# First retention head: values and gates as seven half products round the queries' second turn, weight sums by adding transfers, rotation in other tiles

## The chip, the cores and the metric

The kernel runs on one core of a Trainium2 chip. The metric is the device time of one execution in microseconds; the median of three runs is given. A core has engines that work side by side, each through its own list of instructions in order: TensorE (PE, matmuls; PEld is its weight load), VectorE (DVE), ScalarE (ACT), GpSimd (POOL) and SyncE (SP). The last two serve here to issue transfers, and a transfer issued by POOL may add to what lies at its destination. Engines wait for one another by semaphores.

## The reference

Two layers over 512 rows of 2048 values: forgetting attention with 16 heads, then retention with 8 heads, each with a gate, an output projection, a residual and a layer norm. The change lies in the second layer, at its first head:

```python
def retention_branch(x, w_in, w_out):
    proj = jnp.einsum('bsd,de->bse', x, w_in)
    q, k, v, gate = jnp.split(proj, [RET_QK_WIDTH, 2 * RET_QK_WIDTH, 2 * RET_QK_WIDTH + RET_V_WIDTH], axis=-1)
    q = rotary(q.reshape(B, S, RET_HEADS, RET_QK_DIM))
    k = rotary(k.reshape(B, S, RET_HEADS, RET_QK_DIM)) * (RET_QK_DIM ** -0.5)
    ...
    o = group_norm_heads(o).reshape(B, S, RET_V_WIDTH)
    y = o * jax.nn.silu(gate)
    return jnp.einsum('bse,ed->bsd', y, w_out)
```

Left out above: per head, scores q k^T times a decay, causal, times v, computed by chunks with a running state. A head has 256 columns each of queries and keys and 512 each of values and gates; the input is the normalised output of the first layer, 512 x 2048.

## The kernel before

**Products.** Every projection is a product of the 512 x 2048 input with a block of weights, 2048 x 512 for queries and keys of a head ("narrow") and 2048 x 1024 for gates and values ("wide"). Input and weights are cut into quarters: a11, a12, a21, a22 by half of the rows and half of the 2048 terms, the weights by half of the terms and half of the columns. Each operand is split into a coarse part h and a remainder l (`split`, L303: a ScalarE copy, then a VectorE subtraction), and a product is three matmuls (`mm3`, L308).

**Two kinds of unit.** `Plain` (L643) computes the four result quarters as eight half products. `Unit` (L364) needs seven, p1 to p7, with sums of the input's quarters (the forms s1 to s4, table `FORM`, L38) and of the weights' quarters. Its sums of weights are a chain in one tile of the ring q: quarter 11 for p1, then 12 is added for p5, 22 for p6 and 21 for p4; p7 takes 12 + 22. These additions are VectorE instructions on loaded tiles (`Block.add`, L553). In between results are kept: p2 and p1 (tile k0), p5 (k1) and p1 with p6, called u2, are copied out of their banks by ScalarE (`keep`, L395) and corrected on VectorE when p1, p3 and p7 end (`after`, L430). A half product is four blocks if wide and two if narrow; a wide block is twelve matmuls with 512 columns, a narrow one 24 with 256. In `Plain` each half product is half a result quarter's sum, and wide weights are loaded and split for each half of the rows anew.

**Order.** `Order` (L88) writes out the order of all instructions when the kernel is built. For each block (`slot`, L186) it issues loads up to nine blocks ahead, additions three ahead, splits two ahead and then the block's matmuls. Everything else is a task, a chain of steps; after each block the tasks get one step each (more if a step says wait=0) as long as the planned work of VectorE and ScalarE stays under a limit (L77). Tiles and banks are counted in rings (L74); where a block needs one that isn't free, `require` (L161) forces tasks on until it is. Three accumulators (two banks each) are b0, b1, b2; a unit calls them x, y, z: p1, p6, p7, p4 in x, p2 in y, p5 and p3 in z (`BANK`, L41).

**Around head 0.** The layer norm between the layers ends in `to_columns` (L1424), for each half of the rows: normalise, transpose on TensorE, scale and shift on ScalarE and VectorE, split. The first half gives a11 and a12, the second a21 and a22; the second half's rows are ready only while head 0's first products run. `combine` (L750) splits a21 and a22 and makes s1, s2, s4 and s3, the last only when the second half's plain products have used a21, whose tiles s3 takes (`left_half`, L661). The two banks of queries and keys are copied into tiles in0 and in1 (`take_qk`, L1556), which the last rows of the layer norm hold until their columns are done.

Head 0 has two `Plain` units; they run as queries and keys of the first half of the rows, values and gates of it, queries and keys of the second half, values and gates of it (L1775 to L1778). From head 1 on both are `Unit`s. `attend` (L1579) rotates queries and keys (10 VectorE instructions, two splits), computes scores, multiplies them by the decay table and splits the result; then `take_vg` (L1666) splits the value halves, and `retain` (L1694) does the rest. Tile g2, after head 0's rotation, becomes the room: one half is a fourth tile for raw weights, the other is tile y0 (`split_room`, L333). Head 1's queries use k1 for p1 and p5 and y0 for u2.

Of the kernel before, what the change touches and what calls it, by code (L numbers as in the profile page):

```python
# [11 lines left out]
F32 = mybir.dt.float32  # L12
# [218 lines left out]
def trunk(ctx: ExitStack, tc: tile.TileContext, xq, x, fb_f, columns, wf_in, narrow, wide, ln_g, ln_b, rot, decay,  # L231
# [132 lines left out]
    class Unit:  # L364
# [3 lines left out]
        def __init__(self, w, n, sink, rows=True, u2="k0", p1="k0"):  # L368
# [5 lines left out]
            self.early = False  # L374
# [7 lines left out]
        def accumulator(self, b):  # L382
            if self.tags is None:
                self.tags = dict(zip("xzy", banks))
                banks[:] = banks[1:] + banks[:1]
# [8 lines left out]

        def keep(self, what, bank):  # L395
            n = self.shape[2]
            if self.wide or what == "u2":
                tag = {"p1": self.p1, "p2": "k0", "p5": "k1"}.get(what, self.u2) if self.wide else self.u2
                require(lambda: free[tag])
                take(tag)  # L400
                if tag == "y0":
                    self.pair = in_room(0, [P, 1 if self.wide else 2, 2, n])
                    t = self.pair[:, 0]
                else:
                    t = pool.tile([P, 2, n], F32, name=what, tag=tag)
            else:
                tag = "k1"
                if what == "p1":
                    require(lambda: free[tag])
                    take(tag)  # L410
                    self.p15 = pool.tile([P, 2, 2, n], F32, name="p15", tag=tag)
                    self.p15_users = 2
                t = self.p15[:, int(what == "p5")]
# [73 lines left out]
        def run(self, order=ORDER, then={}, leaves=False, last=False):  # L487
# [6 lines left out]
            i = order.index(("p3", self.blocks - 1))  # L494
# [11 lines left out]
    class Block:  # L506
        before = None

        def __init__(self, unit, p, c, e, shares, shared, then_block, then_product, turned=False):
# [43 lines left out]
        def add(self):  # L553
# [9 lines left out]
            elif p in ("p5", "p6", "p4") and not self.sums:  # L563
# [7 lines left out]
        def split(self):  # L571
# [22 lines left out]
            if p == "p4":  # L594
                give("q")
            if u.early and p == "p6":
# [153 lines left out]
    def combine(rest, plain):  # L750
# [13 lines left out]
        for name in ("s1", "s2"):  # L764
# [10 lines left out]
            if name == "s1":  # L775
                give("g2")
# [747 lines left out]
    class Head:  # L1524
        def __init__(self, h):
# [14 lines left out]
        def first_vg(self, m, n, tile, done):  # L1540

            if m:
                return self.take_vg(m, n, tile, done)
            tag = ("k0", "k1")[n]

            def copy():
                yield need(act=0.97, **{tag: 1})
                take(tag)
                t = pool.tile([P, 2, 512], F32, name="vg_raw", tag=tag)
                nc.scalar.activation(t, tile, AF.Copy)  # L1550
                done()
                self.take_vg(m, n, t, lambda after=0: give(tag, after))

            spawn(copy(), 0)
# [375 lines left out]
```

## Time and profile before

| | before |
|---|---|
| median of three runs (2388.37 to 2389.93) | 2389.52 us |
| the profiled execution | 2388.19 us |
| its span, first to last instruction | 2386.4 us |
| granted clock of TensorE, mean | 0.995 |
| head 0, first value-and-gate block to head 1's first block | 1004.87 to 1127.09 us |
| head 1's stretch | 1127.09 to 1257.82 us |

The profile is of one execution. Rows of engines are: start or count, busy time, line, operation, tile written and tiles read, shape. "[1.23 <-ACT raw L1478]" is idle time of the engine before the instruction and what ended it. Matmuls overlap, so their mean length is longer than the time that one more of them takes. The rows that carry the argument are in the prediction.

### The profile page before, as it was taken

What the parts mean: (1) busy time and instruction counts of PE and PEld (TensorE: products, weight loads), DVE (VectorE), ACT (ScalarE), POOL (GpSimd) and SP (SyncE); (2) the same over time, 40 slices, a digit from 0 to 9 for tenths busy, and PEclk for the clock granted to TensorE, in tenths of its full rate; (3) what the DMA queues carried; (4) which work ended last, traced back from release to release, by engine and by line L of the source; (5) the groups of instructions that cost most, each with busy time, mean ns of one, the idle gap of its engine ahead of it and who ended that gap; (6) DMA issues with size and microseconds to landing.
All of it is one profiled execution on the core that took longest, in us unless ns stands there. A gap on an engine that the chain in (4) does not pass through costs nothing.

```text
span 2386.4 us, 34361 instructions
## 1 busy us (share of the span) xinstructions
PE 2320.9 (97%) x13144; PEld 2016.2 (84%) x13144; DVE 1892.1 (79%) x2480; ACT 1223.0 (51%) x1777; POOL 150.4 (6%) x236
## 2 busy tenths in 40 slices
PE   9999999999999999999999999999999999999995
PEld 9888798798799778788989898988889898777784
DVE  5888778778765655677888888888888889988887
ACT  4546556555554534564454535454545446544533
POOL 0000000000000000000010101010101001011002
PEclk9999999999999999999999999999999999999998
DMA  6355444544544457556675857575655659689778
GB/s 225 123 196 175 163 161 165 183 161 159 190 153 147 135 194 253 190 177 200 203 239 189 247 192 219 198 206 181 212 195 195 211 169 273 212 267 300 238 245 191
DMA packets 185140, 473.26 MB, mean 198 GB/s; under 512 B 18032, under 2 KB 63232, under 8 KB 184464
## 3 DMA queue, kind: packets, MB, share of 16 engines
q1 hardware_dynamic: 161440, 403.68, 50.8%
q0 software_dynamic: 23536, 67.39, 10.7%
q8 instruction: 103, 1.69, 0.3%
q14 instruction: 61, 0.50, 0.1%
HBM read 413.30 MB, written 61.91 MB: 199 GB/s over the span
## 4 chain that ended last, share of the span: by engine, by line
PE 57%; DVE 8%; issue 3%; DMA 3%; ACT 3%; POOL 0%; ACTq 0%; SPq 0%; DVEq 0%; POOLq 0%
PE acc L311 17%; PE acc L312 17%; PE acc L310 17%; DVE w_l L306 3%; ACT w_h L305 2%; PE mmp L310 1%; DMA w_raw<-in_wide 1%; PE mmp L311 1%; PE mmp L312 1%; DVE w_q L565 1%; DMA v_sum<-in_wide 1%; PE mmp L1202 1%; PE mmp L1736 0%; DMA y_s<-ny 0%; DVE z L1835 0%
## 5 line engine op out<-in xcount | busy, mean ns | idle before, releaser
L310 PE MATMUL acc<-w_h,a 128*128 128x512 f32 (+1 forms) x1616 | 581.7, 360 | 5.5 <-DVE p L460 2.9
L311 PE MATMUL acc<-w_l,a 128*128 128x512 f32 (+1 forms) x1616 | 575.9, 356 | 3.7 <-DVE w_l L306 3.7
L312 PE MATMUL acc<-w_h,a 128*128 128x512 f32 (+1 forms) x1616 | 575.6, 356 | 0.0
L305 ACT ACTIVATE w_h<-w_q 128x1024 fp32r<-128x1024 f32 x344 | 363.9, 1059 | 406.3 <-DVE w_q L565 229.2
L306 DVE TENSOR_TENSOR w_l<-w_raw,w_h 128x1024 fp32r<-128x1024 f32 x337 | 411.6, 1222 | 200.9 <-ACT w_h L305 199.6
L305 ACT ACTIVATE w_h<-w_raw 128x1024 fp32r<-128x1024 f32 x337 | 356.3, 1059 | 378.1 <-PE acc L312 171.2
L306 DVE TENSOR_TENSOR w_l<-w_q,w_h 128x1024 fp32r<-128x1024 f32 x344 | 420.1, 1222 | 93.9 <-ACT w_h L305 86.7
L311 PE MATMUL acc<-w_l,s 128*128 128x512 f32 (+1 forms) x1344 | 485.5, 361 | 9.1 <-DVE w_l L306 8.9
L310 PE MATMUL acc<-w_h,s 128*128 128x512 f32 (+1 forms) x1344 | 489.3, 364 | 1.8 <-ACT w_h L305 1.6
L312 PE MATMUL acc<-w_h,s 128*128 128x512 f32 (+1 forms) x1344 | 483.9, 360 | 0.0
L310 PEld LDWEIGHTS acc<-w_h,a 128*128 128x128 f32 x1616 | 305.5, 189 | 48.8 <-issue 4.2
L311 PEld LDWEIGHTS acc<-w_l,a 128*128 128x128 f32 x1616 | 305.7, 189 | 47.7 <-DVE w_l L306 7.0
L312 PEld LDWEIGHTS acc<-w_h,a 128*128 128x128 f32 x1616 | 305.4, 189 | 44.0
L311 PEld LDWEIGHTS acc<-w_l,s 128*128 128x128 f32 x1344 | 254.4, 189 | 51.5 <-DVE w_l L306 16.6
L310 PEld LDWEIGHTS acc<-w_h,s 128*128 128x128 f32 x1344 | 254.4, 189 | 38.0 <-ACT w_h L305 2.1
L312 PEld LDWEIGHTS acc<-w_h,s 128*128 128x128 f32 x1344 | 254.2, 189 | 38.1
L565 DVE TENSOR_TENSOR w_q<-w_q,w_raw 128x1024 f32<-128x1024 f32 x218 | 265.4, 1220 | 9.6 <-DMA w_raw<-in_wide 7.2
L310 PE MATMUL acc<-a,w_h 128*128 128x256 f32 x464 | 131.5, 283 | 1.3 <-ACT w_h L305 1.3
L312 PE MATMUL acc<-a,w_l 128*128 128x256 f32 x464 | 131.6, 284 | 0.8 <-DVE w_l L306 0.8
L311 PE MATMUL acc<-a,w_h 128*128 128x256 f32 x464 | 131.3, 283 | 0.0
L312 PE MATMUL acc<-s,w_l 128*128 128x256 f32 x448 | 126.8, 283 | 0.0
L311 PE MATMUL acc<-s,w_h 128*128 128x256 f32 x448 | 126.7, 283 | 0.0
(244 smaller groups left out, 2942.5 us busy)
## 6 DMA issues: line engine op xcount, KB each, us to landing
w_raw<-in_wide SPq DMA_DIRECT2D x343, 512.0 KB, 3.9
w_raw<-in_narrow SPq DMA_DIRECT2D x146, 512.0 KB, 3.9
w_q<-in_wide SPq DMA_DIRECT2D x60, 512.0 KB, 4.3
room<-in_wide SPq DMA_DIRECT2D x45, 512.0 KB, 4.4
w_q<-in_narrow SPq DMA_DIRECT2D x26, 512.0 KB, 4.3
y_s<-ny POOLq DMA_DIRECT2D x48, 256.0 KB, 7.3
y_s<-y POOLq DMA_DIRECT2D x40, 256.0 KB, 6.2
room<-in_narrow SPq DMA_DIRECT2D x16, 512.0 KB, 4.6
```

The costliest lines, as they stand in the source:

```text
L305: nc.scalar.activation(h, src, AF.Copy)
L306: nc.vector.tensor_sub(l, src, f32(h))
L310: nc.tensor.matmul(ps, a[0], b[0], start=start, stop=False, skip_group_check=True)
L311: nc.tensor.matmul(ps, a[0], b[1], start=False, stop=False, skip_group_check=True)
L312: nc.tensor.matmul(ps, a[1], b[0], start=False, stop=stop, skip_group_check=True)
L565: nc.vector.tensor_add(u.chain[c], u.chain[c], t)
L1202: nc.tensor.matmul(ps[:, k * P:], vh[:, k], pT[:, k, k * P:], start=k == 0, stop=k == ST - 1)
```

## The change

Head 0's values and gates become a `Unit`. It runs in two parts: p2 and p1 after the queries' first turn, the other five after the second turn, p3 and p7 block by block in turn. `combine` follows the query unit. The accumulators of x and z change places in this unit (`between`). Its sums of weights for p5, p6 and p4 are adding transfers on POOL's queue straight from the weights in memory into the tile of ring q, each issued behind the split that last read it (`adds`); the sum for p7 stays on VectorE. The room is made as soon as s1 is split. Head 0's rotation has its tiles in the room and in four of the small ones, and its split queries in g0 and g1; the rotation's steps are cut smaller for all heads, the decay table is loaded ahead of the rotation, and the scores start two blocks sooner after it. Head 1's queries keep p1 and p5 in y0 and u2 in k1, and its values keep p5 in y0.

```diff
@@ Unit
-            self.early = False
+            self.early = self.between = self.adds = False
+            self.p15_tag = self.p5 = "k1"
...
             if self.tags is None:
-                self.tags = dict(zip("xzy", banks))
-                banks[:] = banks[1:] + banks[:1]
+                x, z, y = banks
+                if self.between:
+
+                    x, z = z, x
+                self.tags = dict(x=x, z=z, y=y)
+                banks[:] = z, y, x
...
+        def kept_tile(self, tag):
+            require(lambda: free[tag])
+            take(tag)
+            shape = [P, 2, 2, 256]
+            return in_room(0, shape) if tag == "y0" else pool.tile(shape, F32, name="kept", tag=tag)
+
         def keep(self, what, bank):
             n = self.shape[2]
             if self.wide or what == "u2":
-                tag = {"p1": self.p1, "p2": "k0", "p5": "k1"}.get(what, self.u2) if self.wide else self.u2
...
+                tag = {"p1": self.p1, "p2": "k0", "p5": self.p5}.get(what, self.u2) if self.wide else self.u2
+                t = self.kept_tile(tag)
...
             else:
-                tag = "k1"
+                tag = self.p15_tag
                 if what == "p1":
...
+                    self.p15 = self.kept_tile(tag)
...
-            i = order.index(("p3", self.blocks - 1))
+            i = order.index(("p3", self.blocks - 1)) if ("p3", 0) in order else 0
@@ Block
+            self.comes = u.adds and p in ("p5", "p6", "p4")
...
-            if not self.sums and not shared and p != "p1" and not (turned and p == "p3"):
+            if not self.sums and not self.comes and not shared and p != "p1" and not (turned and p == "p3"):
                 self.quarter = {"p2": "21", "p3": "22", "p4": "21", "p5": "12", "p6": "22", "p7": "12"}[p]
...
-            return -1 if p is None or self.sums or self.again else self.u.of[p, self.c].at
+            return -1 if p is None or self.sums or self.comes or self.again else self.u.of[p, self.c].at
...
-            elif p in ("p5", "p6", "p4") and not self.sums:
+            elif p in ("p5", "p6", "p4") and not self.sums and not self.comes:
                 t = u.lent.pop(("p2", c)) if self.shared else self.t
                 nc.vector.tensor_add(u.chain[c], u.chain[c], t)
...
             if p == "p4":
                 give("q")
+            elif u.adds and p in ("p1", "p5", "p6"):
+                q = {"p1": "12", "p5": "22", "p6": "21"}[p]
+                nc.gpsimd.dma_start(raw.rearrange("p a b -> p (a b)"), u.source(q, c), accum_op=ALU.add)
@@ combine
             if name == "s1":
-                give("g2")
+                if rest:
+                    split_room()
+                else:
+                    give("g2")
@@ Head.__init__ (first_vg goes altogether)
                 self.qk_unit = Plain(narrow, 8, self.take_qk, lambda: [banks[0]] * 2, rows=False)
-                self.vg_unit = Plain(wide, 6, self.first_vg,
-                                     lambda: {(m, n): banks[1 + n] for m in range(2) for n in range(2)})
             else:
                 self.qk_unit = Unit(narrow, 8 + h, self.take_qk, rows=False, u2="y0")
-                self.vg_unit = Unit(wide, 6 + h, self.take_vg, u2="k2")
...
+                if h == 1:
+
+                    self.qk_unit.u2, self.qk_unit.p15_tag = "k1", "y0"
+            self.vg_unit = Unit(wide, 6 + h, self.take_vg, u2="k2")
+            if h == 1:
+                self.vg_unit.p5 = "y0"
@@ Head.attend
         def attend(self):
-            yield need(tmp=4 if self.h == 0 else 2)
+            yield need(tmp=2 if self.h else 4)
             cos, sin = tmp("cos"), tmp("sin")
+            half = None if self.h else [tmp("rope_b") for _ in range(2)]
             nc.sync.dma_start(cos, rot[0])
             nc.sync.dma_start(sin, rot[1])
             by_half = lambda t: t.rearrange("p (m t) -> p m t", m=2)
-            tags = ("k2",) if self.h == 0 else ("in0", "in1")
-            tags_qk = ("g1", "g2") if self.h == 0 else ("g0", "g1")
-            yield need(wait=3, until=lambda: self.have == 4 and all(free[t] for t in tags_qk + tags))
-            for t in tags_qk + tags:
+            tags = ("y0",) if self.h == 0 else ("in0", "in1")
+            tags_qk = "g0", "g1"
+            yield need(wait=3, until=lambda: self.have == 4 and all(free[t] for t in tags_qk + tags + ("d0",)))
+            for t in tags_qk + tags + ("d0",):
                 take(t)
+            dec = pool.tile([P, S], F32, name="dec", tag="d0")
+            nc.sync.dma_start(dec, decay[self.h])
 
             qk = [pool.tile([P, 2, 1024], F32R, name=f"qk_{j}", tag=t) for j, t in zip("hl", tags_qk)]
-            if self.h == 0:
-                half = [by_half(tmp("rope_b")) for _ in range(2)]
-            else:
+            if self.h:
                 self.raw = self.qk_unit.p15, self.qk_unit.pair
 
             for j in range(2):
-                yield need(dve=1.75, wait=0)
+                yield need(dve=1.14, wait=0)
                 raw = self.raw[j]
-                a, *b = (pool.tile([P, 2, 2, 256], F32, name="rope", tag=t) for t in tags)
-                b = [b[0][:, :, e] for e in range(2)] if b else half
+                if self.h:
+                    a, b = (pool.tile([P, 2, 2, 256], F32, name="rope", tag=t) for t in tags)
+                    b = [b[:, :, e] for e in range(2)]
+                else:
+                    a, b = in_room(0, [P, 2, 2, 256]), [by_half(t) for t in half]
                 nc.vector.tensor_mul(a, raw, by_half(cos)[:, :, None, :].to_broadcast([P, 2, 2, 256]))
+                yield need(dve=0.6, wait=0)
                 nc.vector.scalar_tensor_tensor(b[0], raw[:, :, 1], -1.0, by_half(sin), op0=ALU.mult, op1=ALU.mult)
-                yield need(dve=1.85, wait=0)
+                yield need(dve=0.6, wait=0)
                 nc.vector.tensor_mul(b[1], raw[:, :, 0], by_half(sin))
                 for e in range(2):
+                    yield need(dve=0.6, wait=0)
                     nc.vector.tensor_add(a[:, :, e], a[:, :, e], b[e])
                 if j == 1:
-                    for _ in range(4 if self.h == 0 else 2):
+                    for _ in range(2 if self.h else 4):
                         give("tmp")
...
             for t in tags:
                 give(t)
-            yield need(d0=1, in0=1, in1=1)
-            for t in ("d0", "in0", "in1"):
+            yield need(in0=1, in1=1)
+            for t in ("in0", "in1"):
                 take(t)
...
-            dec = pool.tile([P, S], F32, name="dec", tag="d0")
-            nc.sync.dma_start(dec, decay[self.h])
...
-            i, last, wait = 0, [], 3
+            i, last, wait = 0, [], 1
...
             for t in tags_qk:
-                if t == "g2":
-                    split_room()
-                else:
-                    give(t)
+                give(t)
@@ the runs
     first = heads[0]
-    first.qk_unit.run(EACH[0], then={0: lambda: spawn(combine(True, first.vg_unit), 1)})
-    first.vg_unit.run(EACH_N[0])
+    first.qk_unit.run(EACH[0], then={0: lambda: spawn(combine(True, first.qk_unit), 1)})
+    first.vg_unit.between = first.vg_unit.adds = True
+    first.vg_unit.run(FIRST)
     first.qk_unit.run(EACH[1], then={len(EACH[1]) - 1: lambda: spawn(first.attend())})
-    first.vg_unit.run(EACH_N[1], then={len(EACH_N[1]) - 1: lambda: spawn(first.retain())})
+    first.vg_unit.run(REST, then={"p4": lambda: spawn(first.retain())})
```

More of the change, by code (lines that the diff above doesn't have):

```diff
@@ L397, in keep @@
             if self.wide or what == "u2":
-                tag = {"p1": self.p1, "p2": "k0", "p5": "k1"}.get(what, self.u2) if self.wide else self.u2
[L399 to L403, printed above, removed]
-                else:
-                    t = pool.tile([P, 2, n], F32, name=what, tag=tag)
+                tag = {"p1": self.p1, "p2": "k0", "p5": self.p5}.get(what, self.u2) if self.wide else self.u2
+                t = self.kept_tile(tag)
+                if self.wide:
+                    t = t.rearrange("p a b n -> p (a b n)").rearrange("p (a n) -> p a n", a=2)
+                else:
+                    self.pair = t
+                    t = t[:, 0]
             else:
-                tag = "k1"
+                tag = self.p15_tag
                 if what == "p1":
-                    require(lambda: free[tag])
-                    take(tag)
-                    self.p15 = pool.tile([P, 2, 2, n], F32, name="p15", tag=tag)
+                    self.p15 = self.kept_tile(tag)
                     self.p15_users = 2
@@ L1533, in __init__ @@
                 self.qk_unit = Plain(narrow, 8, self.take_qk, lambda: [banks[0]] * 2, rows=False)
-                self.vg_unit = Plain(wide, 6, self.first_vg,
-                                     lambda: {(m, n): banks[1 + n] for m in range(2) for n in range(2)})
             else:
                 self.qk_unit = Unit(narrow, 8 + h, self.take_qk, rows=False, u2="y0")
-                self.vg_unit = Unit(wide, 6 + h, self.take_vg, u2="k2")
[L1540 to L1554, printed above, removed]
+                if h == 1:
[3 more added lines that the diff above has]
+                self.vg_unit.p5 = "y0"
         def take_qk(self, m, n, tile, done):
```

## The prediction, made before the kernel was run

> **What bounds the kernel now.** I read the page first, then the stretches of the first two retention heads, then the waits inside the first one.
>
> ```profile
> span 2386.4 us, 34361 instructions
> PE 2320.9 (97%) x13144; PEld 2016.2 (84%) x13144; DVE 1892.1 (79%) x2480; ACT 1223.0 (51%) x1777; POOL 150.4 (6%) x236
> PE 57%; DVE 8%; issue 3%; DMA 3%; ACT 3%; POOL 0%; ACTq 0%; SPq 0%; DVEq 0%; POOLq 0%
> ```
>
> TensorE is busy nearly throughout and carries the chain that ended last, so a TensorE instruction that goes is worth its time, as long as nothing else is late in its stretch. The next view gives busy time by stretch: the first eight value-and-gate blocks of head 0, the next eight, the second query turn, the last sixteen blocks, then heads 1 and 2 (about 130 us each).
>
> ```profile
> core 0: us, PE busy (x) PEld busy (x) DVE busy (x) ACT busy (x) POOL busy (x), PEclk, DMA share, GB/s
> 1004.87:1034.22 29.35, 26.09 (x120) 19.34 (x118) 15.21 (x18) 19.82 (x34) 0.00 (x0) 1.00 0.43 143
> 1034.22:1057.33 23.11, 22.16 (x96) 18.12 (x97) 20.98 (x20) 16.14 (x18) 0.00 (x0) 1.00 0.63 202
> 1057.33:1080.36 23.03, 23.03 (x193) 23.03 (x192) 18.06 (x16) 11.30 (x11) 0.00 (x0) 1.00 0.56 186
> 1080.36:1127.09 46.73, 46.73 (x212) 38.95 (x211) 34.55 (x35) 23.67 (x25) 0.00 (x0) 1.00 0.67 219
> 1127.09:1257.82 130.73, 130.20 (x750) 114.79 (x749) 114.66 (x146) 63.57 (x75) 13.01 (x20) 1.00 0.67 215
> 1257.82:1388.00 130.18, 129.93 (x747) 114.47 (x746) 113.15 (x140) 63.38 (x74) 13.96 (x22) 1.00 0.68 217
> ```
>
> From 1057 to 1127 TensorE has no idle time at all. It loses time only before about 1036, where the normalised rows of the second half are still being turned into columns; the waits between 1004 and 1130, summed, say for whom:
>
> ```profile
> PE acc L311 <- DVE w_l L306: 1.9, 2, 0.9
> PE mmp L1460 <- ACT raw L1478: 1.6, 2, 1.2
> PE acc L310 <- ACT w_h L305: 0.7, 2, 0.4
> ```
>
> Those 4.2 us come from ScalarE and VectorE handing work to and fro in strict order. POOL has nothing to do from 1004 to 1127.
>
> **The change part by part.** I number head 0's blocks from 0 at 1004.87. Before: 0 to 15 wide, 16 to 23 the second query turn, 24 to 39 wide. After: 0 to 7 wide (p2, p1), 8 to 15 the query turn, 16 to 35 wide (p5, p6, p3 with p7, p4).
>
> *Products.* The head's values and gates are 32 blocks now and 28 after (seven products of four). The price of a block is in the groups between 1080.4 and 1115.7:
>
> ```profile
> L310 PE MATMUL acc<-w_h,a 128*128 128x512 f32 x52 | 20.2, 389 | 0.0
> L311 PE MATMUL acc<-w_l,a 128*128 128x512 f32 x52 | 20.2, 389 | 0.0
> L312 PE MATMUL acc<-w_h,a 128*128 128x512 f32 x52 | 20.2, 389 | 0.0
> ```
>
> Three lines of 52 are 156 matmuls in 35.3 us without idle time: 0.226 us each (the 389 ns overlap), and 2.72 us for a block of twelve. Four blocks are **10.9 us**, all taken from a stretch where TensorE never waits. A narrow block is 23.03 / 8 = 2.88 us.
>
> *A copy in the stretch that is late.* p2 ends after block 3 and is copied out of its bank by ScalarE at once (128x1024). The nearest row is the copy of a raw bank, which the change removes later on, where it was hidden:
>
> ```profile
> L1550 ACT ACTIVATE vg_raw<-acc x2: 1005/1006/1006, 1047.7 to 1058.5; 128x1024 f32<-128x1024 f32 x2
> ```
>
> It is queued ahead of the split of block 6, and from there to block 8 every split is just in time (the waits above). Its ends are 0 and 2.0 (if p1's addition on VectorE, 1.2 us, delays a split as well); I take **+1.0**.
>
> *The query turn finds its bank full.* Both query turns use one bank pair. The copies of the first turn come late, since their tiles are held until the columns are done:
>
> ```profile
> 1034.22 0.50 PE L310 MATMUL acc<-w_h,a 128*128 128x512 f32 x1 [0.43 <-ACT w_h L305]
> 1035.67 0.50 PE L311 MATMUL acc<-w_l,a 128*128 128x512 f32 x1 [0.95 <-DVE w_l L306]
> 1033.12 1.99 ACT L305 ACTIVATE w_h<-w_raw 128x1024 fp32r<-128x1024 f32 x2
> 1035.02 1.06 ACT L1573 ACTIVATE qk_raw<-acc 128x512 f32<-128x512 f32 x2
> ```
>
> Now block 8 is wide, has another bank, and loses 1035.67 - 1034.22 - 0.23 = 1.2 us inside to w_l. After, block 8 is the second turn's first and starts when the copies end, 1035.02 + 1.06 = 1036.1, with its w_l already there: 1.9 lost instead of 1.2, and a little for the handing over: **+0.8** (ends 0, if the copies come one place earlier, and 2.0, if they come behind one more split).
>
> *p5 finds the same bank full.* `between` gives p5 the bank of the queries, so it waits for the second turn's copies:
>
> ```profile
> 1080.36 0.40 PE L310 MATMUL acc<-w_h,a 128*128 128x512 f32 x1
> 1080.44 1.06 ACT L305 ACTIVATE w_h<-w_raw 128x1024 fp32r<-128x1024 f32 x1 [1.82 <-PE acc L311]
> 1081.41 1.06 ACT L1573 ACTIVATE qk_raw<-acc 128x512 f32<-128x512 f32 x2
> ```
>
> Today the next block starts at 1080.36 in other banks while ScalarE does a split and then the copies, up to 1082.47. Kept in this order, p5 starts 2.1 us late, with 0.1 for the handing over **+2.2**. Ends: 1.1 (no split in front) and 3.2 (two). Behind that wait on TensorE stand only p5's own blocks.
>
> *Adding transfers.* Twelve additions of weights for p5, p6 and p4 go to POOL's queue; SP issues 16 loads in place of 32. The only such transfers now are at the end of the kernel (the issues, the landings of w_q<-in_wide, a window there, and a step of the chain of waits there):
>
> ```profile
> w_raw<-in_wide SPq DMA_DIRECT2D x343, 512.0 KB, 3.9
> w_q<-in_wide POOLq DMA_DIRECT2D x4, 512.0 KB, 9.7
> v_sum<-in_wide POOLq DMA_DIRECT2D x4, 512.0 KB, 7.3
> DMA to landing us min/median/max: 6.8/9.7/11.5
> 2310.00:2320.00 10.00, 10.00 (x46) 8.16 (x44) 5.07 (x5) 2.57 (x4) 1.94 (x3) 1.00 1.03 340
> 2323.71 13.79 DMA v_sum<-in_wide
> ```
>
> The 6.8 to 11.5 us were taken with the DMA engines full (1.03); here their share is about 0.6. The narrowest place is p5 to p6, four blocks apart. A split starts when the block three ahead of it has ended, and both halves are done about 2.7 us later; the same tile's next split must start 1.06 us before its block, so 6 x 2.72 - 1.1 - 2.7 = 12.5 us are left for the transfer. I take **0**; ends 0 and 1.3 (a landing of 13.8, as in the last row). The four follow each other by a block, so a late one is paid once. p1 to p5 has the query turn between, p6 to p4 eight blocks. POOL's queue holds nothing else then, so its waits hold up nobody.
>
> By the Trainium skill ("SBUF — State Buffer", SBUF: two separate sides) a transfer issued from POOL cannot get its descriptors written while VectorE runs a two-port operation, and 0.62 us became 3.1 in its example; by that figure, an estimate, the slowest landing would be 11.5 + 2.5 = 14.0 and the sum 1.5 us worse. So far the trace speaks against it, as here:
>
> ```profile
> 1180.00:1200.00 20.00, 20.00 (x95) 16.51 (x94) 18.72 (x20) 13.49 (x18) 4.32 (x8) 1.00 0.55 193
> ```
>
> Eight issues took 4.32 us, 0.54 each, beside a VectorE that was busy 18.72 of 20.
>
> *VectorE and ScalarE.* Four pairs of splits go (w_h, w_l); four sums for p7 and three corrections with a bank (p1, p3, p7) come on VectorE, and three bank copies replace two on ScalarE.
>
> ```profile
> L306 DVE TENSOR_TENSOR w_l<-w_raw,w_h 128x1024 fp32r<-128x1024 f32 x32 | 39.1, 1224 | 16.7 <-ACT w_h L305 16.6
> ```
>
> From 1034.22 to 1127.09 VectorE works 20.98 + 18.06 + 34.55 = 73.6 of 92.9 us. After: 73.6 + 3 x 1.22 = 77.2 of 92.9 - 10.9 + 3.0 - 0.7 = 84.3, or 92%. Heads 1 and 2 run at 88% and 87% with 0.5 and 0.25 us of idle TensorE, so I take 0; beyond them the cover is thin (a rival below).
>
> *Forms.* p5, p6, p3 and p7 need s1, s2, s4 and s3, so far needed only by head 1. The second halves of s1 and s4 are split at
>
> ```profile
> 1046.22 1.22 DVE L306 TENSOR_TENSOR s<-raw,s 128x1024 fp32r<-128x1024 f32 x1
> 1074.09 1.22 DVE L306 TENSOR_TENSOR s<-raw,s 128x1024 fp32r<-128x1024 f32 x1
> ```
>
> that is in blocks 12 and 22: one step of the combining a block from block 8 on, sixteen in all. s3 no longer waits for the last wide blocks. So s1 is there by block 12 (needed 16), s2 by 16 (20), s4 by 22 (24), s3 by 24 (25): no wait, one block of room at the narrowest.
>
> *Rotation and scores.* The same VectorE instructions, other tiles, smaller portions; the decay table (256 KB on SP) is loaded ahead. They move from free blocks beside the full ones. The smaller portions, the earlier table and the two blocks less of pause hold for the later heads too, where TensorE idles so little that they can win almost nothing; I take 0 for all of it, with the cover as just said.
>
> **Sum:** -10.9 + 1.0 + 0.8 + 2.2 = **-6.9 us** on the profiled execution's 2388.19 us (span 2386.4 and 1.8 around): 2381.3. The median of the runs shown, 2389.52, lies 1.3 above that execution, so **2382.6 us**. The ends of the unknown terms give -10.9 + 1.1 = -9.8 and -10.9 + 2.0 + 2.0 + 3.2 + 1.3 = -2.4, or 2379.7 to 2387.1.
>
> **The rivals.**
>
> *Nothing of it is waited for.* ScalarE's copies fit into its idle time and the better supply of weights also takes away most of the 4.2 us of waits: -10.9 - 1 gives 2377.6; with p5's wait alone 2380. For it: ScalarE is busy 19.8 of 29.4 us. Against: its order is strict. 0.15.
>
> *VectorE becomes the bound.* If it can be used only to the 88% of head 1, 77.2 us take 87.7 instead of 84.3: 3.4 us, 2386.0. For it: in the stretch of p3 and p7 the rotation comes on top of splits and sums. Against: what is late can go on into head 1. 0.15.
>
> *The transfers are late, or the copies stand behind more.* The upper ends above, and landings some 3 us longer: 2385 to 2390. 0.1.
>
> *The saving moves.* TensorE gets to head 1 earlier and waits there for head 0's attention: 2389. 0.08.
>
> *Slower: head 1 stops at tile k1.* Head 1's queries put their p6 into k1, which is free only when head 0's second value half is split, after all rotation and scores. Today that takes from the first row to the end of the second:
>
> ```profile
> 1090.99 1.22 DVE L1602 TENSOR_TENSOR rope<-qk_raw,cos 128x1024 f32<-128x1024 f32 x1
> 1140.23 1.22 DVE L306 TENSOR_TENSOR v_l<-acc,v_h 128x1024 fp32r<-128x1024 f32 x1
> 1137.51 0.60 ACT L415 ACTIVATE p<-acc 128x512 f32<-128x512 f32 x1 [1.60 <-DVE v_l L306]
> 1115.75 0.39 PE L310 MATMUL mmp<-qk_h 128*128 128x512 f32 x1
> ```
>
> 1090.99 to 1141.45 is 50.5 us, and a copy of head 1 already waits for the first value half (third row; the fourth is the first of the scores). After, rotation can start when s3 is split (block 24), and k1 is wanted 12 x 2.72 + 6 x 2.88 = 50 us later, plus some 4 us of scores. For the change: the pause between rotation and scores shrinks by two blocks, 5.4 us. If it is not done by then, the order must put the rest ahead of everything, with no blocks between: half of the 25.7 us from the first scores to the last value split, some 12 us, so 2382.6 + 12 = 2395. It decides from about 9 us of delay on. 0.12. (By the Trainium skill, "TensorE: Matmul & The Clock Gate", Part 1, an idle window of about 3.4 us halves the clock; by it the 12 us would grow by some 3. The trace has the clock at 1.00 beside idle times up to 1.64 us, and nothing as long.)
>
> **Chances.** Forecast 0.40; the others as given. About 0.2% (4.8 us) is what a measurement of this kernel can tell from no change. Faster by over 0.2% (under 2384.7): the forecast, the first rival and a share of the second and third, 0.62. Within: 0.27. Slower (over 2394.3): 0.11. The range from 2377.5, the first rival, to 2391, past the late transfers, leaves out the slower case and a little below.
>
> **What would show it.** Right: 28 blocks, head 1's first query block near 1127 - 6.9 = 1120; an idle of about 2 us before p5 put down to ScalarE's copies; one of about 2 us before block 8; accumulating landings of 6 to 10 us; no wait of a split for them. Wrong: idle TensorE between blocks 20 and 48, put down to VectorE or to a transfer on POOL; issues of POOL over 1.2 us; a wait at head 1's first copies; other gaps opening after head 1.

## The result: 0.7% slower, and the profile after

The changed kernel takes 2404.14 us (median of four runs, 2403.45 to 2408.25), the kernel before 2388.94 beside it (four runs, 2387.13 to 2389.93). The ratio is 1.0068, with a 95% interval of 1.0051 to 1.0085. The prediction was 2382.6 with a range to 2391; the time lies beyond it, on the other side.

The first two lines of the page after:

```profile
span 2401.7 us, 34231 instructions
PE 2320.4 (97%) x13096; PEld 2014.9 (84%) x13096; DVE 1894.4 (79%) x2483; ACT 1216.2 (51%) x1774; POOL 160.7 (7%) x248
```

48 matmuls are gone, as meant, and yet TensorE's busy time is the same to 0.5 us. So some of what is left runs slower, and 15 us of span came on top. Where, the stretches show (columns as in the prediction). Of before, the first is head 0 from its first query block to head 1's first, the second is head 7 and the output projections:

```profile
979.02:1127.09 148.07, 143.05 (x818) 123.95 (x819) 108.14 (x121) 83.13 (x101) 2.13 (x4) 1.00 0.60 201
...
1904.67:2386.43 481.76, 449.04 (x2133) 371.49 (x2131) 415.12 (x491) 233.80 (x249) 49.69 (x70) 0.98 0.78 236
```

The same of after, with heads 1 and 3 between:

```profile
978.67:1120.42 141.75, 134.04 (x758) 117.01 (x759) 108.28 (x121) 78.55 (x96) 12.68 (x16) 0.96 0.70 198
1120.42:1269.96 149.54, 135.28 (x762) 118.67 (x760) 117.95 (x149) 64.88 (x76) 13.04 (x20) 0.94 0.60 185
...
1399.56:1529.16 129.60, 129.54 (x744) 114.11 (x742) 112.42 (x140) 62.66 (x73) 11.97 (x17) 1.00 0.68 206
...
1917.96:2401.67 483.71, 451.85 (x2133) 373.97 (x2131) 415.01 (x491) 232.96 (x249) 49.43 (x70) 0.97 0.78 235
```

| stretch | before | after | difference |
|---|---|---|---|
| up to head 0 | 979.02 | 978.67 | -0.35 |
| head 0 | 148.07 | 141.75 | -6.32 |
| head 1 | 130.73 | 149.54 | **+18.81** |
| heads 2 to 6 | 646.85 | 648.00 | +1.15 |
| head 7 and after | 481.76 | 483.71 | +1.95 |
| span | 2386.43 | 2401.67 | +15.24 |

Head 0's sum came out as forecast: head 1 starts at 1120.42, forecast near 1120. Part of that is luck, since terms that were wrong made up for one another (see the table under why the prediction was wrong). Head 1 then loses 18.8 us. The timeline of TensorE in the kernel after has these waits (start, length, instruction, idle time before it and what ended it):

```profile
1036.20 0.58 PE L310 MATMUL acc<-a,w_h 128*128 128x256 f32 x1 [3.11 <-ACT qk_raw L1576]
...
1062.82 0.67 PE L310 MATMUL acc<-w_h,s 128*128 128x512 f32 x1 [2.05 <-ACT qk_raw L1576]
...
1191.06 0.65 PE L1740 MATMUL mmp<-ident,kept 128*128 128x128 f32 x4 [1.76 <-ACT kept L1753]
1196.83 1.12 PE L1740 MATMUL mmp<-ident,kept 128*128 128x128 f32 x4 [5.12 <-ACT kept L1753]
1204.72 0.79 PE L310 MATMUL mmp<-qk_h 128*128 128x512 f32 x1 [6.78 <-ACT ny L1745]
```

The first two are the waits for the bank of the queries, before block 8 and before p5. The last three, 13.7 us, are a **stop in head 1**, between its seventh and eighth value-and-gate block; TensorE has no idle time in the 126 us from p5's start to it. Each of the waits has a second price, in the granted clock (PEclk, the number behind POOL's busy time; rows of stretches of the kernel after):

```profile
1036.20:1039.12 2.92, 2.91 (x13) 2.92 (x14) 2.92 (x3) 1.50 (x2) 0.00 (x0) 0.50 0.76 244
...
1062.82:1066.40 3.58, 3.58 (x9) 2.81 (x10) 1.37 (x2) 0.00 (x0) 0.87 (x1) 0.52 0.95 168
...
1192.60:1209.70 17.10, 6.09 (x16) 4.62 (x17) 12.45 (x21) 6.27 (x8) 2.16 (x4) 0.50 0.54 161
1209.70:1216.00 6.30, 6.30 (x29) 5.23 (x28) 2.52 (x4) 3.03 (x3) 0.29 (x1) 0.99 0.36 103
```

TensorE runs at half its clock for 2.9 and 3.6 us behind the short waits and for 17.1 us in the stop. In the kernel before the whole of 979 to 1258 has 1.00.

What the engines did in the stop. VectorE, in the kernel after:

```profile
1197.46 1.23 DVE L1609 TENSOR_TENSOR rope<-kept,cos 128x1024 f32<-128x1024 f32 x1
1198.60 0.68 DVE L1611 SCALAR_TENSOR_TENSOR rope<-kept,sin 128x512 f32<-128x512 f32 x1
1199.20 0.68 DVE L1613 TENSOR_TENSOR rope<-kept,sin 128x512 f32<-128x512 f32 x1
1199.81 1.29 DVE L1616 TENSOR_TENSOR rope<-rope 128x512 f32<-128x512 f32 x2
1202.21 1.23 DVE L306 TENSOR_TENSOR qk_l<-rope,qk_h 128x1024 fp32r<-128x1024 f32 x1 [1.12 <-ACT qk_h L305]
```

and ScalarE:

```profile
1195.11 1.06 ACT L305 ACTIVATE qk_h<-rope 128x1024 fp32r<-128x1024 f32 x1 [4.10 <-DVE rope L1616]
1196.07 0.71 ACT L1753 ACTIVATE kept<-kept,gn_r 128x512 f32<-128x512 f32 x1
1201.12 1.06 ACT L305 ACTIVATE qk_h<-rope 128x1024 fp32r<-128x1024 f32 x1 [4.35 <-DVE rope L1616]
1202.09 0.58 ACT L1744 ACTIVATE y<-mmp 128x512 f32<-128x512 f32 x1
...
1205.18 1.01 ACT L423 ACTIVATE kept<-acc 128x1024 f32<-128x1024 f32 x1
```

This is the rotation of head 1 (L1609 to L1616, the split of qk) in turn with `retain` of head 0 (L1753 scales a gate, L1740 transposes it, L1744 copies it), step by step, with no block of products between, and at the end a copy of an accumulator: `keep` of head 1's p1. It goes into tile k0, which holds head 0's first gate half until the third of `retain`'s six transposing steps has used it. `require` forced both tasks on until k0 was free. Only `retain` was needed; the rotation's steps came along, and ScalarE and TensorE stood behind them.

The adding transfers, in the kernel after (all uses of tile w_q from 1004 to 1120; the first row has the time of an issue, min/median/max in ns), and the wait of TensorE for splits there:

```profile
L608 POOL DMA_DIRECT2D w_q<-in_wide x12: 863/876/911, 1018.6 to 1081.5; - x12
...
DMA to landing us min/median/max: 3.6/5.5/7.8
```

```profile
PE acc L311 <- DVE w_l L306: 0.9, 2, 0.6
```

All additions landed within 7.8 us, and the 0.9 us of waits fall at 1026.92 and 1030.29, ahead of block 8, in blocks whose weights aren't sums.

### The profile page after: what moved, and what is told of

It reads as the page before. It is cut to its first block, busy times and chain, and to the rows that moved or that the text cites. A ratio compares the mean times of both kernels' runs of the same rounds, so it can differ in the third digit from the quotient of the medians.

```text
span 2401.7 us, 34231 instructions
## 1 busy us (share of the span) xinstructions
PE 2320.4 (97%) x13096; PEld 2014.9 (84%) x13096; DVE 1894.4 (79%) x2483; ACT 1216.2 (51%) x1774; POOL 160.7 (7%) x248
## 4 chain that ended last, share of the span: by engine, by line
PE 44%; DVE 5%; DMA 3%; issue 2%; ACT 1%; POOL 0%; ACTq 0%; DVEq 0%; POOLq 0%
PE acc L310 13%; PE acc L311 13%; PE acc L312 13%; DVE w_l L306 2%; DMA w_raw<-in_wide 2%; PE mmp L310 1%; PE mmp L311 1%; PE mmp L312 1%; DVE w_q L575 1%; ACT w_h L305 1%; PE mmp L1740 0%; DVE z L1840 0%; DMA y_s<-ny 0%; DMA y_s<-y 0%; DMA z_half<-z_in 0%
## 5 line engine op out<-in xcount | busy, mean ns | idle before, releaser
L305 ACT ACTIVATE w_h<-w_q 128x1024 fp32r<-128x1024 f32 x360 | 380.4, 1059 | 425.5 <-DVE w_q L575 218.3
L310 PE MATMUL acc<-w_h,a 128*128 128x512 f32 (+1 forms) x1536 | 551.4, 359 | 6.2 <-DVE kept L468 3.5
L311 PE MATMUL acc<-w_l,a 128*128 128x512 f32 (+1 forms) x1536 | 545.3, 355 | 1.8 <-DVE w_l L306 1.8
L306 DVE TENSOR_TENSOR w_l<-w_raw,w_h 128x1024 fp32r<-128x1024 f32 x314 | 383.4, 1222 | 206.2 <-ACT w_h L305 205.3
L312 PE MATMUL acc<-w_h,a 128*128 128x512 f32 (+1 forms) x1536 | 545.1, 355 | 0.0
L306 DVE TENSOR_TENSOR w_l<-w_q,w_h 128x1024 fp32r<-128x1024 f32 x360 | 439.3, 1221 | 118.1 <-ACT w_h L305 111.1
L310 PE MATMUL acc<-w_h,s 128*128 128x512 f32 (+1 forms) x1408 | 515.9, 366 | 4.3 <-ACT qk_raw L1576 2.1
L311 PE MATMUL acc<-w_l,s 128*128 128x512 f32 (+1 forms) x1408 | 512.0, 364 | 8.0 <-DVE w_l L306 7.9
L312 PE MATMUL acc<-w_h,s 128*128 128x512 f32 (+1 forms) x1408 | 510.1, 362 | 0.0
L305 ACT ACTIVATE w_h<-w_raw 128x1024 fp32r<-128x1024 f32 x314 | 331.7, 1058 | 346.7 <-PE acc L312 161.5
L310 PEld LDWEIGHTS acc<-w_h,a 128*128 128x128 f32 x1536 | 290.9, 189 | 48.3 <-issue 7.4
L312 PEld LDWEIGHTS acc<-w_h,a 128*128 128x128 f32 x1536 | 290.8, 189 | 41.2
L311 PEld LDWEIGHTS acc<-w_l,s 128*128 128x128 f32 x1408 | 267.6, 190 | 51.4 <-DVE w_l L306 13.6
L310 PEld LDWEIGHTS acc<-w_h,s 128*128 128x128 f32 x1408 | 267.5, 190 | 44.1 <-ACT w_h L305 3.0
L312 PEld LDWEIGHTS acc<-w_h,s 128*128 128x128 f32 x1408 | 267.4, 190 | 41.2
```

What stands on the lines that cost most here:

```text
L305: nc.scalar.activation(h, src, AF.Copy)
L306: nc.vector.tensor_sub(l, src, f32(h))
L310: nc.tensor.matmul(ps, a[0], b[0], start=start, stop=False, skip_group_check=True)
L311: nc.tensor.matmul(ps, a[0], b[1], start=False, stop=False, skip_group_check=True)
L312: nc.tensor.matmul(ps, a[1], b[0], start=False, stop=stop, skip_group_check=True)
```

## The experiments

The theory after the result: (1) the small portions of the later heads' rotation let it run ahead of `retain` wherever VectorE has 0.6 us left in a turn, so k0 is late; (2) both waits for the queries' bank are real and cost more than their idle time. Rivals: the stop comes from the head being 6.7 us earlier, whatever the portions (1'); the waits for the bank only stand in for others that would come in their place (2').

**e1: portions of heads 1 to 7 as before, in `attend`.**

```diff
-                yield need(dve=1.14, wait=0)
+                yield need(dve=1.75 if self.h else 1.14, wait=0)
...
-                yield need(dve=0.6, wait=0)
+                if not self.h:
+                    yield need(dve=0.6, wait=0)
...
-                yield need(dve=0.6, wait=0)
+                yield need(dve=1.85 if self.h else 0.6, wait=0)
...
-                    yield need(dve=0.6, wait=0)
+                    if not self.h:
+                        yield need(dve=0.6, wait=0)
```

> The changed kernel, with the rotation of heads 1 to 7 in its former portions (two steps a half, planned at 1.75 and 1.85 us, in place of five); head 0 as changed. Theory (the small portions fill VectorE's planned budget in head 1, so that head 0's last steps come late, tile k0 is not free when head 1's values want it, and the order forces five turns with nothing on TensorE): the idle time of 1.8 + 5.1 + 6.8 us between 1189 and 1205 goes, and with it 17 us at half clock, in which TensorE worked some 5: 13.7 + 2.6 = 16.3 us less than the changed kernel, about 2388. Rival (VectorE is short around head 1 whatever the portions are, since head 0's work has become denser): the stop only moves, and the time stays within 4 us of 2404.

Measured: 2389.83 us (ten runs, 2385.99 to 2392.17) beside 2389.31 of before (thirty runs), ratio 1.0001 (0.9992 to 1.0011). The stop is gone; head 1 in this kernel:

```profile
1119.92:1254.92 135.00, 132.76 (x761) 116.40 (x760) 115.97 (x147) 64.02 (x76) 12.45 (x19) 1.00 0.62 197
```

The head still starts at 1119.92, so 1' falls. Of the 13.7 us nothing is left; two other waits, of 1.1 and 1.2 us, stand later in the head (at 1211.34 and 1235.04).

**e2: the second query turn in another bank** (that of p2, which its early copy has left).

```diff
-                self.qk_unit = Plain(narrow, 8, self.take_qk, lambda: [banks[0]] * 2, rows=False)
+                self.qk_unit = Plain(narrow, 8, self.take_qk, lambda: [banks[0], banks[2]], rows=False)
```

> The changed kernel, with the second query turn in the bank that p2 has left in place of the first turn's. Theory (the waits before block 8 and before p5 are for copies out of one bank, and each brings 3.4 us at half clock): idle times of 3.1 and 2.1 us go, and two spells of half clock, 1.7 us each; some 1.2 us of waits for the splits of blocks 8 and 9 come back: 7 us less, about 2397, with the stop in head 1 as long as before. Rival (TensorE only gets sooner to the forced turns in head 1, whose end VectorE and ScalarE set): under 2 us less, about 2403.

Measured: 2395.70 us (seven runs, 2394.04 to 2396.81), ratio 1.0027 (1.0016 to 1.0038). Heads 0 and 1 of this kernel:

```profile
977.09:1111.93 134.84, 131.20 (x758) 114.63 (x759) 108.08 (x121) 78.59 (x96) 12.67 (x16) 0.99 0.72 208
1111.93:1261.01 149.08, 134.82 (x762) 118.31 (x760) 117.97 (x149) 64.87 (x76) 12.98 (x20) 0.95 0.60 185
```

Head 0 takes 134.84 in place of 141.75 us: 4.1 us less idle (3.64 against 7.71) and 2.8 less busy time for the same 758 matmuls, half clock that is gone. So the waits were worth 6.9 us, and 2' falls. One half-clock step of the three in head 0 is left: the one at the head's first products, ahead of these waits. (The profiled executions are 9.4 us apart, the medians 8.4; 1.6 of that arose ahead of head 0, which starts sooner here by as much, and the kernels of this study scatter there from 976.95 to 979.49.) The stop in head 1 stays whole (149.08).

**e3: both of these.**

> Both edits. Theory: the two are independent, 2404 - 16.3 - 7 = 2381, that is 8 us under the kernel before and near what the change was forecast to give. Rival (VectorE short around head 1): 2390 or more, with waits of TensorE for w_l in head 1.

Measured: 2383.57 us (eleven runs, 2380.67 to 2386.34), ratio 0.9979 (0.9971 to 0.9988). The two gains nearly add up (14.3 and 8.4 less than after make 2381.4); head 1 keeps waits as in e1 (135.74 us, 2.9 of them idle).

**e7: is it the tile?** The small portions stay. Head 1's values run p1, p2 and p5 block by block in turn, so that p1 ends, and wants k0, three blocks later.

```diff
+THREE = (("p1", "p2", "+p5"), ("p6",), ("p3", "p7"), ("p4",))
...
-        h.vg_unit.run(leaves=h.h == RH - 1,
+        h.vg_unit.run(THREE if h.h == 1 else ORDER, leaves=h.h == RH - 1,
```

> The changed kernel with the small portions kept; only head 1's values run p1, p2 and p5 in turns of one block each, so that p1 ends three blocks later and tile k0 is wanted some 8 us later. Theory (tile k0): the stop goes although the portions are the same, 2387 to 2390. Rival (the portions delay all of VectorE's work, whichever tile): the stop stays or moves to another tile, 2398 or more.

Measured: 2387.77 us (ten runs, 2384.72 to 2389.53), ratio 0.9992 (0.9983 to 1.0001). Head 1:

```profile
1120.35:1252.48 132.13, 132.03 (x762) 116.58 (x760) 116.15 (x149) 63.60 (x76) 12.40 (x19) 1.00 0.66 216
```

The same 762 matmuls in 132.13 us, 0.1 of them idle. The same work of VectorE over the head fits (116.15 of 132.13, 88%), with the portions still small: it was the order within the head, not the amount.

But e7 moves more than the need. VectorE's timelines show when `retain` has its second pair of scale factors (gn_r), behind which its transposing steps follow, and when the rotation of head 1 begins (cos). In the kernel after:

```profile
1177.37 1.22 DVE L1609 TENSOR_TENSOR rope<-room,cos 128x1024 f32<-128x1024 f32 x1
...
1194.31 0.17 DVE L1733 TENSOR_SCALAR gn_r<-gn_r 128x2 f32<-128x2 f32 x1
```

in e1:

```profile
1182.88 0.17 DVE L1735 TENSOR_SCALAR gn_r<-gn_r 128x2 f32<-128x2 f32 x1
...
1187.79 1.22 DVE L1609 TENSOR_TENSOR rope<-room,cos 128x1024 f32<-128x1024 f32 x1
```

and in e7:

```profile
1180.47 0.17 DVE L1734 TENSOR_SCALAR gn_r<-gn_r 128x2 f32<-128x2 f32 x1
...
1181.68 1.22 DVE L1610 TENSOR_TENSOR rope<-room,cos 128x1024 f32<-128x1024 f32 x1
```

In the kernel after the rotation went first; in both experiments `retain` did, in e7 too, although the portions are small. ScalarE's rows give the room that is left at k0: the start of the scaling that stands last in the step of `retain` that frees k0 (the third row of its kind), and the start of p1's copy into k0.

| kernel | k0 free, about | copy into k0 | room |
|---|---|---|---|
| before | 1187.49 | 1197.01 | 9.5 |
| f5 (below) | 1186.36 | 1195.46 | 9.1 |
| after | 1204.57 | 1205.18 | none: wanted from 1189.3 |
| e1 | 1189.04 | 1189.84 | 0.8 |
| e7 | 1185.75 | 1199.38 | 13.6 |

So in e7 k0 was free 3.5 us before the moment at which the kernel after wanted it. The later need was not put to the test by itself, and e1 has just room enough. What both runs show is that the stop goes when `retain` gets its turns ahead of the rotation. Why it gets them in e7 is read from the kernel and not shown by a run of its own: with p2's blocks in between, an addition of weights falls on every third block in place of every second, so that more is left of VectorE's limit in a turn.

**f1: e2 and e7 together.**

> The changed kernel with the second query turn in p2's bank and head 1's values in the order p1, p2, p5; portions small as changed. Theory (three independent terms: product, bank waits with their half-clock windows, stop at k0): 2387.8 of the reordered kernel less the 6.2 to 8.4 us that the bank was worth in the two runs with it: 2380 to 2381.6. Rival (the two edits overlap): 2384 or more.

Measured: 2381.08 us (five runs, 2378.06 to 2381.88) beside 2390.01 of before (fifteen runs, one of them 2915.25 us and left out of the ratios), ratio 0.9958 (0.9945 to 0.9970).

**f2: f1, and for heads 1 to 7 the decay table and the pause as before.** This asks what the 0.3 us is by which each later head is longer.

```diff
-            dec = pool.tile([P, S], F32, name="dec", tag="d0")
-            nc.sync.dma_start(dec, decay[self.h])
+            if self.h == 0:
+                dec = pool.tile([P, S], F32, name="dec", tag="d0")
+                nc.sync.dma_start(dec, decay[self.h])
...
+            if self.h:
+                dec = pool.tile([P, S], F32, name="dec", tag="d0")
+                nc.sync.dma_start(dec, decay[self.h])
...
-            i, last, wait = 0, [], 1
+            i, last, wait = 0, [], 3 if self.h else 1
```

> As the run before, but heads 1 to 7 load the decay table behind the rotation and pause three blocks before the scores, as the kernel before did. Heads 2 to 7 took 129.26 us each before and 129.57 to 129.60 in every kernel with the change. Theory (the shorter pause costs 0.3 us a head): 129.26 again and 2 us less. Rival (it is the small portions, or only the order in which products fall between blocks): no change in head 2 to 7, within 1 us.

Measured: **2378.52 us** (five runs, 2377.60 to 2379.16), ratio 0.9949 (0.9937 to 0.9962): the lowest median of all, with a range that overlaps those of f1 and of f4 below. What shows the gain is the length of the later heads. (Before, heads 3 to 7 took 129.26 us each and head 2 took 129.81.) Head 3 in f1,

```profile
1373.81:1503.41 129.60, 129.54 (x743) 114.11 (x742) 112.53 (x140) 62.66 (x73) 11.99 (x17) 1.00 0.66 205
```

and head 3 in f2, behind the stretch of head 0's late values:

```profile
1062.00:1124.00 62.00, 62.00 (x315) 53.03 (x314) 56.67 (x56) 30.92 (x32) 4.40 (x5) 1.00 0.64 174
...
1374.68:1503.94 129.26, 129.26 (x743) 114.18 (x742) 112.61 (x140) 62.69 (x73) 12.00 (x17) 1.00 0.65 206
```

**f5: the kernel before, with only the later heads' portions, table and pause of the change.**

```diff
-            yield need(wait=3, until=lambda: self.have == 4 and all(free[t] for t in tags_qk + tags))
+            yield need(wait=3, until=lambda: self.have == 4 and all(free[t] for t in tags_qk + tags + (("d0",) if self.h else ())))
...
-                yield need(dve=1.75, wait=0)
+                yield need(dve=1.14 if self.h else 1.75, wait=0)
...
-                yield need(dve=1.85, wait=0)
+                yield need(dve=0.6 if self.h else 1.85, wait=0)
...
-            i, last, wait = 0, [], 3
+            i, last, wait = 0, [], 1 if self.h else 3
```

> The kernel before, with only what the change does to heads 1 to 7: small portions of the rotation, table ahead, the shorter pause; head 0 as before. Theory (the stop needs the earlier head 1 and the small portions together): no stop, within 3 us of the kernel before, 2389 to 2392, later heads at 129.6 us. Rival (the portions alone make the stop at k0): 10 us or more over it.

Measured: 2390.16 us (eleven runs, 2389.02 to 2395.08), ratio 1.0003 (0.9994 to 1.0012), head 1 130.33 us, no stop. So the three changes to the later heads, on the kernel before, make no stop: it takes the change around head 0 too. Its later heads are 129.57 us long against 129.26 before, as in f1. The 0.3 us thus go with the earlier table and the shorter pause, and with neither the products nor the portions; which of the two costs them, and why, the runs don't say (in the kernel after, a matmul of head 3 starts 0.2 us late, at 1510.00, and the profile shows nothing that it waited for).

**f4: f2 with e1's portions too.**

> The second of these, with the rotation's portions of heads 1 to 7 as before too: later heads are then wholly as before, and only head 0, the second query turn's bank and head 1's order of products differ. Theory: within 1 us of that run, since after the reordering no block waits for k0 whatever the portions are. Rival (the portions still cost in head 1): 2 us or more less.

Measured: 2380.36 us (five runs, 2378.37 to 2382.39), ratio 0.9957 (0.9945 to 0.9970). That is 1.8 more than f2, with ranges that overlap: not decided. Its head 0 has no half clock at all:

```profile
979.49:1114.03 134.54, 130.34 (x758) 113.15 (x759) 108.08 (x121) 78.59 (x96) 12.67 (x16) 1.00 0.73 209
```

A version with the sums of weights back on VectorE was not tried, so what the adding transfers win or lose against it stays open.

## Why the prediction was wrong

Term by term, in us of the profiled executions:

| term | predicted | measured |
|---|---|---|
| four blocks of products | -10.9 | -10.9 |
| p2's copy, other waits before block 8 | +1.0 | -1.0 |
| block 8 finds the bank full | +0.8 | +1.7 |
| p5 finds the bank full | +2.2 | +2.05 |
| half clock in head 0 | none | +3.7 |
| twelve matmuls that move from head 0 to head 1 | none | -1.8, +1.8 |
| head 1: idle, half clock | 0 | +13.7, +3.25 |
| heads 2 to 6 | 0 | +1.15 |
| head 7 and after | 0 | +1.95 |

*Products.* Right. Head 0 has 60 matmuls fewer; 48 are the four blocks, twelve now run in head 1 (762 against 750). At the full clock head 0's 758 take 130.34 us busy (f4), 12.7 less than before; e7's head 1 takes 132.03, 1.8 more than before.

*p2's copy.* Wrong in sign: the other waits between 1004 and block 8 went from 2.83 us to 1.80, as the first rival had it for this place.

*The bank.* The mechanism was right at both places. At block 8 the copies started when the forecast had them (1035.08, forecast 1035.02); TensorE, which had waited less until then, came 0.7 us sooner (1033.09 against 1033.79) and so stood longer. The errors of this term and of the one before are thus in part one and the same: ScalarE's copies set when block 8 starts, and what TensorE lost or saved just before didn't move it. ScalarE's timeline of the kernel after:

```profile
1034.13 1.05 ACT L305 ACTIVATE w_h<-w_raw 128x1024 fp32r<-128x1024 f32 x1
1035.08 1.07 ACT L1576 ACTIVATE qk_raw<-acc 128x512 f32<-128x512 f32 x2
...
1060.74 1.06 ACT L305 ACTIVATE w_h<-w_q 128x1024 fp32r<-128x1024 f32 x1 [0.87 <-ACT s L305]
1061.70 1.06 ACT L1576 ACTIVATE qk_raw<-acc 128x512 f32<-128x512 f32 x2
```

The size failed at the clock, which the sum left out: 134.04 - 130.34 = 3.7 us for three half-clock windows in head 0, two of them behind these waits (2.8 us, which e2 won back) and one at the head's first products (below). The prediction weighed the clock only in its slower rival, for 12 us; for its own waits of about 2 us it left it out, though the trace had shown 1.00 beside "idle times up to 1.64 us" and nothing longer.

*Transfers, forms, VectorE's load.* Right at 0. Nothing waits from 1066 to 1189, and f2 runs VectorE at 56.67 of 62 us, 91%, with TensorE never idle, so the rival in which VectorE may be used to 88% only falls. POOL's issues took 0.88 us each (the 0.54 of the prediction were of transfers half as large) and held up nothing. Both views have VectorE at work almost only with TENSOR_TENSOR and SCALAR_TENSOR_TENSOR instructions, so what another kind of VectorE operation does to an issue was not seen.

*The step that failed* is "The smaller portions, the earlier table and the two blocks less of pause hold for the later heads too, where TensorE idles so little that they can win almost nothing; I take 0 for all of it". They could not win, but they could lose, and the step never asked. The cover that it named is VectorE's load over a stretch; what gave way was the order of two tasks in it. A step of 0.6 us often fits into what is left of the limit (4.4 us of VectorE, L77) where a step of `retain` (1.2 to 1.45) doesn't, so the later task went first: in the order as written, the last six blocks ahead of the stop have two steps of `retain` and four of the rotation, and with e1's portions six and one. `retain` of head 0 had also less room: four blocks fewer lie ahead of the place where k0 is wanted, and in the order as written it starts only one block sooner.

*The slower rival* had the right mechanism, an order that forces tasks on for a tile that isn't free, and a chance of 0.12. It named the wrong tile: k1, wanted by head 1's queries, for which nothing waited. It was k0, one unit later, kept not by a value half but by a gate half. Its price, 12 us, was near the 13.7 of idle time; the half clock put 3.25 on top (it had said "some 3"). That the price fitted is luck, since it was worked out for another tile. A list of every tile that head 1 needs from head 0, each with the step that frees it, should have brought up k0: its room in the kernel before was 9.5 us, of which 2.6 are left when head 1 starts 6.9 us sooner and `retain` stays where it is.

*The later heads and the end.* +1.15 goes with the table and the pause (f2 has 129.26 again; from f1 to f2 the medians gain 2.6 us, the five heads of this row 1.7). At the end two waits that were there before grew from 1.55 to 1.86 and from 1.64 to 2.02 us, each now followed by half clock: busy time there is 451.85 against 449.04, idle time 0.9 less. f2 loses at the same places (485.2 us from head 7 on), and that is left unmended.

*Luck.* Head 1 began where it was forecast because -2.0 us (p2's copy), -1.8 (matmuls that moved to head 1) and -0.2 (p5) nearly made up for +3.7 (the clock) and +0.9 (block 8).

With the stop and the bank waits mended and the table and the pause as before, f2 gains 11.5 us on before (2390.01 - 2378.52), slightly more than the four blocks.

## What to carry to other kernels

Where a planner hands out an engine's spare time step by step, cutting a task's steps smaller is a change of priority: ask which larger steps of another task now come later, and which tile they free. When work moves forward, list every buffer that the next stage takes over, with the instruction that frees each, not only the one that comes first. A wait of 2 us on TensorE may cost up to 1.7 us more in clock than its own length (half of a step of 3.4 us; the three steps in head 0 cost 3.7 together), so a bank that is full "for only two microseconds" deserves another bank.

## What the hardware showed

The clock halves after much shorter idle times than I had assumed. In each trace the half-clock spells begin and end on one grid of 3.41 us, and last a whole number of its steps (3.4, 6.8, 13.7, 17.1; only the last of each trace, which runs past the kernel's last instruction, isn't such a number). When TensorE's idle times are summed in each step of that grid, between 200 and 2360 us in ten traces, every step with 1.86 us of idle time or more is followed by a half-clock step, and no step at full clock with up to 1.70 us is. (Two steps that were themselves at half clock had less than 1.86 us and were followed by another: 0.76 us in f1 at 2328.9, which stays unexplained, and 1.78 us in the kernel after at 1202.9.) Between, 1.74 (e3) and 1.76 (after, f5) are followed by one, and 1.76 (e2) and 1.80 (e7) aren't. So about half of a step decides. The Trainium skill ("TensorE: Matmul & The Clock Gate", Part 1) has the free-running window of 3413 ns, which these traces show, but speaks of a whole idle window before the clock drops; here half a window was enough, and the measurement decides.

So the same wait can be free or not, by where it falls. The first products of head 0, before:

```profile
979.02 0.39 PE L310 MATMUL acc<-a,w_h 128*128 128x256 f32 x1 [1.25 <-ACT w_h L305]
...
980.28 0.39 PE L312 MATMUL acc<-a,w_l 128*128 128x256 f32 x1 [0.76 <-DVE w_l L306]
```

and after:

```profile
978.67 0.39 PE L310 MATMUL acc<-a,w_h 128*128 128x256 f32 x1 [1.19 <-ACT w_h L305]
...
979.93 0.39 PE L312 MATMUL acc<-a,w_l 128*128 128x256 f32 x1 [0.76 <-DVE w_l L306]
```

The waits are alike, 2.0 us in all. Before, the grid cuts them apart (1.24 us in one step), and the clock stays; after, 1.76 us fall into one step. The stretch behind them, before,

```profile
980.90:984.50 3.60, 3.60 (x31) 3.48 (x30) 3.60 (x5) 1.32 (x2) 0.00 (x0) 1.00 0.52 162
```

and after:

```profile
981.10:984.50 3.40, 3.40 (x18) 3.40 (x17) 3.40 (x5) 0.58 (x1) 0.00 (x0) 0.50 0.51 164
```

That is 18 matmuls in 3.4 us against 31 in 3.6. That the threshold is half a step was read from these traces, not made to happen in a run of its own.
